# Attention with two exponential engines: loads by need, blank matmuls ahead of the scores, and longer VectorE chains from later jobs

## The chip, the cores and the metric

The kernel runs on one core of one Trainium2 chip. The metric is the device time of one execution in microseconds; lower is better. Before the change the median of 7 runs is 397.64 us (397.14 to 398.09).

## The reference

Grouped-query attention: 8 batches, 8 query heads, 2 key/value heads (each serves 4 query heads), 1024 positions, head size 64, float32 in and out.

```python
scores = scale * np.matmul(q_group, k_group.transpose(0, 1, 3, 2))
attn = np.exp(scores - np.max(scores, axis=-1, keepdims=True))
attn = attn / (np.sum(attn, axis=-1, keepdims=True) + 1e-08)
output[:, q_start:q_end, :, :] = np.matmul(attn, v_group)
```

The kernel leaves out the subtraction of the maximum (the scores are small) and the 1e-08.

## The kernel before, in words

**Jobs and cells.** A job is a batch, a head and a side: the even or the odd query rows of that head, 512 of them. There are 128 jobs, and each has 8 cells, one for each block of 128 keys: 1024 cells. A cell passes through a score matmul (128 keys by 512 queries, L351), an exponential, and four output matmuls (L414), which multiply the weights by V with a column of ones beside it, so that the sum of the weights comes out as a 65th column. When the eight cells of a job are done, `normalise` takes the reciprocal of that column (L427), multiplies (L429) and stores (L435, on SP's queue).

**Two ways to the exponential.** Cells of kind A go in pairs to ACT: one ACTIVATE over 128x1024 (L362). Cells of kind D go to DVE: L371 turns the score into the bits of a bfloat16 power of two, and when `GROUP` cells (four) have been gathered in one tile, a chain of four instructions over all of them mends the mantissa: an AND (L386), a line (L392), a product (L402) and an integer addition (L406). In PSUM, A has two slots of two banks, D two banks, and the outputs two banks; a bank is free again when its reader is done.

**The order.** `make_plan` plays the engines through with a table of costs and writes the order out: which score, exp, L371, chain step, output matmul and norm comes when. Each engine then runs its instructions strictly in that order, and waits by semaphores where data or a buffer isn't there. Cells are taken one after the other, the next one by whichever kind has a free bank first. Loads are put into the same list at due times before a head's first use (`first_use`).

**Loads.** `cast` (L248, POOL's queue) copies Q, K or V of a head from DRAM to a scratch in bfloat16, and is paced by a dependency on the latest score at that point of the list. `transpose` (L260, SP's queue) brings Q or K back transposed, in two pieces. `place_k` (L268, POOL's queue) copies the transposed K to the halves of `kset`; there K stands in one half of the partitions and zeros in the other, since `qT` holds the even rows in its lower and the odd rows in its upper half. There are two `kset`s, for even and odd batches; the zeros are set once, one set's by DVE (L236), the other's by POOL (L309). `place_v` (L282) is on SP's queue.

**The first head** (`first_loads`) takes a shorter way: K and Q come as float32 in one DMA each (L294), DVE casts K (L313, L314), ACT casts Q (L316), PE turns both (L321, L327), and DVE and ACT copy them from PSUM (L330 to L334).

Of the kernel before, what the change touches and what calls it, by code (L numbers as in the profile page):

```python
# [13 lines left out]

GROUP = 4


def make_plan(nj, nkc):
# [5 lines left out]

    QK, PV, EXP, P1, NORM = 0.214, 0.143, 0.925, 0.605, 0.57
    CHAIN = (0.73, 0.73, 1.26, 1.26)
    FROM_PE, FROM_ACT, FROM_DVE = 0.28, 0.18, 0.12
    LIVE_A, LIVE_D, PENDING, ONLY_A = 26, 6, 8, 14
    INF = 1e9
    n = nj * nkc  # L30
    ops = []
    pe = act = dve = 0.0
    a_free, bank, obank_free = [0.0, 0.0], [0.0, 0.0], [0.0, 0.0]
    nxt = 0
    open_jobs, next_job, rem, obank = [], 0, {}, {}
# [5 lines left out]
    a_id = d_id = -1  # L41

    def first_free(slots):
        return min(range(len(slots)), key=lambda s: slots[s])

    while normed < nj:
        best = None
        if nxt < n:
            ta = td = INF
            if open_a is not None:  # L50
                ta = max(pe, open_a["t"])
            elif live["A"] < LIVE_A:
                ta = max(pe, min(a_free))
            if pending < PENDING and nxt < n - ONLY_A and (cur or live["D"] < LIVE_D):
                td = max(pe, min(bank))
            t, to_d = (ta, 0) if ta <= td else (td, 1)
            if t < INF:
                best = min(best or (INF,), (t, 1 + to_d, "qk", to_d))
        for i, s in enumerate(open_jobs):
            for c in rem[s]:  # L60
                at = max(pe, ready.get(s * nkc + c, INF))
                if at < INF:
                    best = min(best or (INF,), (at, 3 + i, "pv", (s, c)))
        if len(open_jobs) < 2 and next_job < nj:
            at = max(pe, min(obank_free), min(ready.get(next_job * nkc + c, INF) for c in range(nkc)))
            if at < INF:
                best = min(best or (INF,), (at, 3 + len(open_jobs), "open", next_job))
        for q, p, kind in ((normq, 0, "norm"), (p1q, 1, "p1"), (chainq, 2, "chain")):
            if q:
                best = min(best or (INF,), (max(dve, q[0][0]), p, kind, 0))  # L70
        if cur and nxt >= n - ONLY_A and not p1q:
            best = min(best or (INF,), (dve, 9, "flush", 0))
        t, _, kind, arg = best
        if kind == "qk":
            cell = nxt
            nxt += 1
            pe = t + QK
            if not arg:
                if open_a is None:
# [8 lines left out]
                home[cell] = ("A", a_id)  # L88
                if len(o["cells"]) == 2 or nxt >= n:
                    act = max(act, pe + FROM_PE)  # L90
                    ops.append((act, "exp", a_id, tuple(o["cells"])))
                    act += EXP * len(o["cells"]) / 2
                    a_free[o["slot"]] = act + FROM_ACT
                    uses[("A", a_id)] = len(o["cells"])
                    for x in o["cells"]:
                        ready[x] = act + FROM_ACT
                    open_a = None
            else:
                k = first_free(bank)
                bank[k] = INF  # L100
# [44 lines left out]
        elif kind == "flush":  # L145
            chainq.append((dve, d_id, cur, 0))
            cur = []
        else:
            _, g, cells, step = chainq.pop(0)
            ops.append((t, "chain", g, len(cells), step))  # L150
            dve = t + CHAIN[step] * len(cells) / GROUP
            if step + 1 < len(CHAIN):
                chainq.insert(0, (dve, g, cells, step + 1))
            else:
                pending -= len(cells)
                uses[("D", g)] = len(cells)
                for x in cells:
                    ready[x] = dve + FROM_DVE
# [4 lines left out]
def kernel(  # L163
# [26 lines left out]
    E1 = D + 1  # L190
    PIECE = 256
    scale = 1.0 / math.sqrt(D)
    bits_scale = 128.0 * scale * math.log2(math.e)
# [13 lines left out]
    first_pool = ctx.enter_context(tc.tile_pool(name="firstp", bufs=1))  # L207
    qT_pool = ctx.enter_context(tc.tile_pool(name="qTpool", bufs=8))
    kT_pool = ctx.enter_context(tc.tile_pool(name="kTpool", bufs=4))
    pa_pool = ctx.enter_context(tc.tile_pool(name="papool", bufs=26))  # L210
    pd_pool = ctx.enter_context(tc.tile_pool(name="pdpool", bufs=6))
    tmp_pool = ctx.enter_context(tc.tile_pool(name="tmppool", bufs=2))
# [11 lines left out]
    apools, dbanks, obanks = psum_pools("aps", 2), psum_pools("dps", 2), psum_pools("ops", 2)  # L224

    ident = const_pool.tile([128, 128], BF16)
    make_identity(nc, ident)
    vsets, ksets = [], []
    for s in range(2):
# [4 lines left out]
        for side in range(2):  # L234
            if s == 0:
                nc.vector.memset(ks[(1 - side) * D : (2 - side) * D, :, side, :], 0.0)  # L236
        ksets.append(ks)
# [51 lines left out]
    def first_loads():  # L289

        staged = []
        for eng, src in ((nc.sync, k[0, 0]), (nc.scalar, q[0, 0])):
            f = first_pool.tile([128, NHC, 2, D], FP32, name=f"f{len(staged)}")
            eng.dma_start(  # L294
                out=f, in_=src.rearrange("(c p two) d -> p c two d", p=128, two=2)
            )
            staged.append(f)
        vf = first_pool.tile([128, NHC, 2, D], FP32, name="vf")
        nc.sync.dma_start(
            out=vf, in_=v[0, 0].rearrange("(c p two) d -> p c two d", p=128, two=2)  # L300
        )
        cast(("q", 0, 1), q[0, 1])
        for two in range(2):
# [3 lines left out]
            )  # L307
        for side in range(2):
            nc.gpsimd.memset(ksets[1][(1 - side) * D : (2 - side) * D, :, side, :], 0.0)  # L309
        fk, fq = staged  # L310

        hk = first_pool.tile([128, NHC, 3, D], BF16, name="hk")
        nc.vector.tensor_copy(out=hk[:, :, 0:2, :], in_=fk)  # L313
        nc.vector.tensor_copy(out=hk[:, :, 2, :], in_=fk[:, :, 0, :])  # L314
        hq = first_pool.tile([128, NHC, 2 * D], BF16, name="hq")
        nc.scalar.copy(out=hq, in_=fq.rearrange("p c two d -> p c (two d)"))  # L316
        tk = dbanks[0].tile([128, 2, HALF], BF16, name="dps0")
        tq = dbanks[1].tile([128, HALF], BF16, name="dps1")
        for w in range(2):
            for c in range(NHC):  # L320
                nc.tensor.transpose(  # L321
                    tk[:, w, c * 128 : (c + 1) * 128],
                    hk[:, c, w : w + 2, :].rearrange("p w d -> p (w d)"),
                    ident,
                )
        for c in range(NHC):
            nc.tensor.transpose(tq[:, c * 128 : (c + 1) * 128], hq[:, c, :], ident)  # L327
        qT[(0, 0)] = qT_pool.tile([128, HALF], BF16, name="qT")
        lo, hi = slice(0, D), slice(D, 2 * D)
        nc.vector.tensor_copy(out=ksets[0][lo, 0, 0, 0:HALF], in_=tk[lo, 0, :])  # L330
        nc.scalar.copy(out=qT[(0, 0)], in_=tq)
        nc.vector.tensor_copy(out=ksets[0][lo, 0, 0, HALF:S], in_=tk[lo, 1, :])
        nc.vector.tensor_copy(out=ksets[0][hi, 0, 1, 0:HALF], in_=tk[hi, 1, :])
        nc.vector.tensor_copy(out=ksets[0][hi, 0, 1, HALF:S], in_=tk[hi, 0, :])  # L334

# [113 lines left out]
    for op in plan:  # L449
        if op[1] == "qk":  # L450
            first_use.setdefault(op[2] // NKC, op[0])
        at(op[0], run[op[1]], *op[2:])
    for b in range(B):
        for h in range(H):
            if b == 0 and h == 0:
                continue
            th = first_use[(b * H + h) * 2]
            if (b, h) != (0, 1):
                at(th - 28.0, cast, ("q", b, h), q[b, h])
            for n in range(HALF // PIECE):  # L460
                at(th - 17.0 + n, transpose_q, b, h, n)
            if h % HPG == 0:
                g = h // HPG
                at(th - 38.0, cast, ("k", b, g), k[b, g])
                at(th - 33.0, cast, ("v", b, g), v[b, g])
                for n in range(HALF // PIECE):
                    at(th - 27.0 + n, transpose_k, b, g, n)
                for side in range(2):
                    for parity in range(2):
                        at(th - 20.0, place_k, b, g, side, parity)  # L470
                at(th - 15.0, place_v, b, g)
    with tc.manual_schedule():
# [33 lines left out]
```

The softmax here doesn't subtract the row's maximum and nothing guards it: scores larger than these inputs give would overflow.

## Time and profile before

| | us |
|---|---|
| median of 7 runs | 397.64 |
| the profiled execution | 397.68 |
| its span, first to last instruction | 395.9 |
| ACT busy | 381.5 |
| DVE busy | 376.0 |
| PE busy | 371.6 |
| POOL busy | 86.8 |
| first exp on ACT begins | 8.27 |
| last exp on ACT ends | 388.53 |

Busy times are sums over the profiled execution. A busy PE is not PE at its peak, since matmuls overlap and their ends are modelled. Lines of a timeline give the start, the time from the first instruction of the row to the end of its last, the engine, the line of the kernel, the operation, what it writes and reads, and how many instructions of the kind follow each other; in brackets is the idle time before the row and what ended it. Lines of a group give the busy time, the mean duration of one in ns, and the idle time before them. Lines of windows give the stretch and its length, then busy time and instructions of PE, PE's weight loads, DVE, ACT and POOL, then the granted clock of PE, the share of time that the DMA engines are busy, and GB/s.

### The profile page before, as it was taken

How to read it: one execution, taken by the hardware profiler on the slowest of the kernel's cores; microseconds unless marked ns; L12 is line 12 of the kernel's file. 1: busy time of each engine (PE TensorE's matmuls, PEld its weight loads, DVE VectorE, ACT ScalarE, POOL GpSimd, SP SyncE). 2: the span in 40 equal slices, each digit the busy share in tenths (PEclk: the TensorE clock that was granted, in tenths of full speed). 3: DMA queues.
4: the chain of work that ended last, by engine and by line, in shares of the span. 5: the costliest groups of instructions: out<-in, count | busy, mean ns of one | idle time of the engine just before them, and what ended most of it. 6: DMA issues, size and time to landing. Idle time of an engine off the chain costs nothing.

```text
span 395.9 us, 12772 instructions
## 1 busy us (share of the span) xinstructions
PE 371.6 (94%) x5132; PEld 232.9 (59%) x5132; DVE 376.0 (95%) x664; ACT 381.5 (96%) x415; POOL 86.8 (22%) x165
## 2 busy tenths in 40 slices
PE   4899999999999999999999999999999999999996
PEld 2455565565656656665656565565665666565655
DVE  4999999999999999999999999999999999999995
ACT  4999999999999999999999999999999999999992
POOL 5340403131041313113131040311213131120000
PEclk9999999999999999999999999999999999999999
DMA  4694967758586796857658576785965967564314
GB/s 106 106 141 89 164 112 140 133 102 135 100 133 124 119 150 113 134 96 137 117 106 137 104 150 119 128 128 98 160 107 112 156 127 118 108 126 97 68 28 94
DMA packets 134890, 46.72 MB, mean 118 GB/s; under 512 B 130848, under 2 KB 132384, under 8 KB 133344
## 3 DMA queue, kind: packets, MB, share of 16 engines
q1 hardware_dynamic: 129408, 29.52, 38.6%
q0 software_dynamic: 4896, 16.13, 27.0%
q8 instruction: 40, 0.66, 0.8%
q10 hardware_dynamic: 528, 0.26, 0.2%
q14 instruction: 18, 0.15, 0.1%
HBM read 27.13 MB, written 28.97 MB: 142 GB/s over the span
## 4 chain that ended last, share of the span: by engine, by line
ACT 71%; PE 9%; DVE 8%; issue 6%; DMA 4%; POOL 1%; SPq 1%
ACT pa L362 71%; PE aps L351 4%; PE ops L414 4%; DMA qT<-scr_q 2%; DVE y L402 2%; DVE pd L371 1%; DVE pd L406 1%; DVE ost L429 1%; DMA vf<-in_v_dram 1%; PE dps L351 1%; POOL kset L309 1%; DVE y L392 1%; DMA scr_q<-in_q_dram 1%; DVE z L386 1%; DVE rec L427 1%
## 5 line engine op out<-in xcount | busy, mean ns | idle before, releaser
L362 ACT ACTIVATE pa<-aps 128x1024 bf16<-128x1024 f32 x412 | 379.0, 1063 | 2.4 <-PE aps L351 1.6
L351 PE MATMUL aps<-qT,kset 128*128 128x512 bf16 x824 | 245.3, 379 | 14.0 <-ACT pa L362 11.9
L414 PEld LDWEIGHTS <-pa 128*128 128x128 bf16 x3296 | 134.6, 97 | 57.6 <-DVE ost L429 0.8
L414 PE MATMUL ops<-vset,pa 128*128 128x65 bf16 x3296 | 143.9, 193 | 0.0
L371 DVE TENSOR_SCALAR pd<-dps 128x512 uint16<-128x512 f32 x200 | 129.8, 682 | 2.3 <-PE dps L351 2.3
L351 PEld LDWEIGHTS <-kset 128*128 128x128 bf16 x1024 | 85.2, 97 | 66.4 <-issue 30.9
L248 POOL DMA_DIRECT2D scr_q<-in_q_dram x63 | 34.7, 550 | 174.8 <-PE aps L351 153.3
L351 PE MATMUL dps<-qT,kset 128*128 128x512 bf16 x200 | 64.5, 380 | 0.1
L406 DVE TENSOR_TENSOR pd<-pd,y 128x2048 uint16<-128x2048 uint16 x50 | 61.2, 1225 | 1.7
L402 DVE TENSOR_TENSOR y<-z,y 128x2048 f16<-128x2048 uint16 x50 | 61.2, 1225 | 1.7
L429 DVE TENSOR_TENSOR ost<-ops,rec 128x256 f32<-128x256 f32 x128 | 54.3, 425 | 4.4
L414 PEld LDWEIGHTS <-pd 128*128 128x128 bf16 x800 | 38.5, 97 | 30.0 <-DVE pd L406 8.1
L268 POOL DMA_DIRECT2D kset<-kT x60 | 31.9, 540 | 73.7 <-DMA kT<-scr_k 70.8
L414 PE MATMUL ops<-vset,pd 128*128 128x65 bf16 x800 | 45.3, 194 | 1.4 <-DVE pd L406 0.3
L392 DVE TENSOR_SCALAR y<-z 128x2048 f16<-128x2048 uint16 x50 | 34.3, 687 | 0.6
L386 DVE TENSOR_SCALAR z<-pd 128x2048 uint16<-128x2048 uint16 x50 | 34.3, 685 | 0.0
L427 DVE RECIPROCAL rec<-ops 128x4 f32<-128x4 f32 x128 | 22.5, 176 | 2.5 <-PE ops L414 1.9
L248 POOL DMA_DIRECT2D scr_k<-in_k_dram x15 | 8.1, 541 | 6.6 <-PE aps L351 5.7
L248 POOL DMA_DIRECT2D scr_v<-in_v_dram x15 | 7.5, 503 | 8.1 <-PE aps L351 7.0
L321 PE MATMUL dps<-ident,hk 128*128 128x128 bf16 x8 | 1.0, 308 | 5.1 <-DVE hk L313 5.1
L321 PEld LDWEIGHTS <-hk 128*128 128x128 bf16 x8 | 0.8, 138 | 5.1 <-DVE hk L313 5.1
L309 POOL MEMSET kset<- 64x2048 bf16 x2 | 3.6, 1798 | 0.1
(20 smaller groups left out, 9.7 us busy)
## 6 DMA issues: line engine op xcount, KB each, us to landing
out_dram<-ost SPq DMA_DIRECT2D x128, 128.0 KB, 3.1
scr_q<-in_q_dram POOLq DMA_DIRECT2D x63, 128.0 KB, 3.3
kset<-kT POOLq DMA_DIRECT2D x60, 64.0 KB, 2.7
qT<-scr_q SPq DMA_TRANSPOSE x126, 3.7
scr_k<-in_k_dram POOLq DMA_DIRECT2D x15, 128.0 KB, 4.2
scr_v<-in_v_dram POOLq DMA_DIRECT2D x15, 128.0 KB, 4.0
vset<-scr_v SPq DMA_DIRECT2D x30, 64.0 KB, 4.1
kT<-scr_k SPq DMA_TRANSPOSE x30, 3.2
```

The costliest lines, as they stand in the source:

```text
L248: dma = nc.gpsimd.dma_start(out=scr.rearrange("(p f) -> p f", f=1024), in_=src.rearrange("(p s) d -> p (s d)", s=1024 // D),)
L268: nc.gpsimd.dma_start(out=ksets[b % 2][side * D : (side + 1) * D, g, side, parity * HALF : (parity + 1) * HALF], in_=kT[(b, g)][parity * D ...
L351: last_score[0] = nc.tensor.matmul(dst, lhsT=ksets[b % 2][:, h // HPG, side, c * 128 : (c + 1) * 128], rhs=qT[(b, h)], start=True, stop=Tr ...
L362: nc.scalar.activation(out=pt[:, 0:m], in_=psum.pop(("A", n))[:, 0:m], func=AF.Exp, scale=scale)
L371: nc.vector.tensor_scalar(out=groups[g][:, slot], in0=psum.pop(cell), scalar1=bits_scale, scalar2=bits_bias, op0=ALU.mult, op1=ALU.add,)
L386: nc.vector.tensor_scalar(out=z, in0=pd, scalar1=0x7F, scalar2=None, op0=ALU.bitwise_and)
L392: nc.vector.tensor_scalar(out=y, in0=temps[g][0], scalar1=CURVE_A / 128.0, scalar2=CURVE_B, op0=ALU.mult, op1=ALU.add,)
L402: nc.vector.tensor_tensor(out=y, in0=z, in1=y, op=ALU.mult)
L406: nc.vector.tensor_tensor(out=pd, in0=pd, in1=y, op=ALU.add)
L414: nc.tensor.matmul(ops_of[s][:, qs, :], lhsT=p_of[cell][:, qs * 128 : (qs + 1) * 128], rhs=vsets[b % 2][:, h // HPG, c, :], start=opens an ...
L427: nc.vector.reciprocal(out=rec, in_=o[:, :, D])
L429: nc.vector.tensor_tensor(out=ost, in0=o[:, :, 0:D], in1=rec.unsqueeze(2).to_broadcast([128, NQS, D]), op=ALU.mult,)
```

## The change

- `GROUP` is 8: the four chain steps run over 4096 elements for each partition. There are 5 such tiles for 6 of the smaller ones, and 28 `pa` tiles for 26.
- The planner has new costs (a fixed part and a part for each cell). A cells are taken in the order of jobs; D cells are taken from jobs up to `LEAD` = 6 further on (fewer at the start), at most two of a job. A scores get precedence by 0.08 us in its clock. It counts on the loads of a head from a given time on.
- The first K and Q come in two DMAs each, and are cast, turned and copied by halves. 26 matmuls of a blank tile go ahead of the first transposes on PE, and two more between the halves. The third part of K's cast and the four transposes that need it come after the first copies to `kset`, still ahead of the first score.
- All four memsets of zeros are on DVE, at the start; POOL has none. The cast of the third head's Q goes out after the blank matmuls, paced by them.
- Loads have due times that are closer at the start and farther later, and the casts are sorted by them.

The order of the built kernel: 411 exps for 412, 202 cells on DVE for 200 (25 chains of eight cells and one of two, for 50 of four), 5160 matmuls for 5132.

```diff
-GROUP = 4
+GROUP = 8
...
-    QK, PV, EXP, P1, NORM = 0.214, 0.143, 0.925, 0.605, 0.57
-    CHAIN = (0.73, 0.73, 1.26, 1.26)
-    FROM_PE, FROM_ACT, FROM_DVE = 0.28, 0.18, 0.12
-    LIVE_A, LIVE_D, PENDING, ONLY_A = 26, 6, 8, 14
+    QK, PV, P1, NORM = 0.216, 0.1225, 0.603, 0.555
+    EXP, AND, LINE, PRODUCT = (0.065, 0.4265), (0.20, 0.133), (0.20, 0.133), (0.16, 0.27)
+    CHAIN = (AND, LINE, PRODUCT, PRODUCT)
+    FROM_PE, FROM_ACT, FROM_DVE, FROM_POOL = 0.26, 0.17, 0.10, 0.15
+    LIVE_A, LIVE_D, PENDING, PER_JOB, LEAD, RAMP, AHEAD, FIRST_PV = 28, 5, 16, 2, 6, 3, 0.08, 2.0
...
+        while job_a < nj and not todo[job_a]:
+            job_a += 1
+        lead = min(LEAD, job_a // RAMP)
+        job_d = max(job_d, job_a + lead)
+        while job_d < nj and (
+            taken[job_d] >= PER_JOB or not todo[job_d]
+        ):
+            job_d += 1
...
+                best = min(best or (INF,), (t - AHEAD, 1, "qk", 0, t))
+        if job_d < nj and job_d <= job_a + lead + 1 and pending < PENDING:
+            if cur or live["D"] < LIVE_D:
+                t = max(pe, min(bank), loaded(job_d))
...
+    blank = const_pool.tile([128, 128], BF16)
+    nc.vector.memset(blank, 0.0)
...
         for side in range(2):
-            if s == 0:
-                nc.vector.memset(ks[(1 - side) * D : (2 - side) * D, :, side, :], 0.0)
+            nc.vector.memset(ks[(1 - side) * D : (2 - side) * D, :, side, :], 0.0)
...
-        for side in range(2):
-            nc.gpsimd.memset(ksets[1][(1 - side) * D : (2 - side) * D, :, side, :], 0.0)
...
+        for eng, f, src in ((nc.sync, fk, k[0, 0]), (nc.scalar, fq, q[0, 0])):
+            for half in halves:
+                eng.dma_start(
+                    out=f[:, half], in_=src.rearrange(rows, p=128, two=2)[:, half]
+                )
...
+        last_score[0] = keep_warm(WARM)
+        for n, half in enumerate(halves):
+            nc.vector.tensor_copy(out=hk[:, half, 0:2, :], in_=fk[:, half])
+            nc.scalar.copy(
+                out=hq[:, half], in_=fq[:, half].rearrange("p c two d -> p c (two d)")
+            )
+            turn_k(0, half)
+            for c in range(NHC)[half]:
+                nc.tensor.transpose(tq[:, c * 128 : (c + 1) * 128], hq[:, c, :], ident)
+            if n == 0:
+                keep_warm(2)
+                cast(("q", 0, 2), q[0, 2])
+        for half in halves:
+            cols = slice(half.start * 128, half.stop * 128)
+            nc.scalar.copy(out=qT[(0, 0)][:, cols], in_=tq[:, cols])
+            put_k(0, 0, half)
+        nc.vector.tensor_copy(out=hk[:, :, 2, :], in_=fk[:, :, 0, :])
+        turn_k(1, slice(0, NHC))
+        put_k(0, 1, slice(0, NHC))
+        put_k(1, 0, slice(0, NHC))
+        put_k(1, 1, slice(0, NHC))
...
-                at(th - 28.0, cast, ("q", b, h), q[b, h])
+            spare = min(1.0, max(0.0, th - 10.0) / 50.0)
+                casts.append((th - 12.0 - 14.0 * spare, ("q", b, h), q[b, h]))
...
+    casts.sort(key=lambda e: e[0])
```

## The prediction

> **What bounds the kernel now.** I read the shares and the windows first, then the groups, then the timeline at both ends, where the windows show the slack.
>
> ```profile
> PE 371.6 (94%) x5132; PEld 232.9 (59%) x5132; DVE 376.0 (95%) x664; ACT 381.5 (96%) x415; POOL 86.8 (22%) x165
> ```
>
> ```profile
> 0.00:10.00 10.00, 4.24 (x20) 2.35 (x21) 4.42 (x9) 4.21 (x5) 5.55 (x13) 1.00 0.40 105
> ...
> 100.00:200.00 100.00, 96.74 (x1344) 61.05 (x1343) 97.46 (x172) 99.77 (x110) 22.26 (x41) 1.00 0.70 120
> ...
> 380.00:396.00 16.00, 11.07 (x225) 8.10 (x221) 11.09 (x22) 8.54 (x10) 0.00 (x0) 0.97 0.34 71
> ```
>
> The columns are PE, PEld, DVE, ACT, POOL. Three engines look full on average, but in the middle only ACT leaves nothing (99.77 of 100 us); DVE and PE wait for it. ACT is idle only at the ends. The groups give the prices:
>
> ```profile
> L362 ACT ACTIVATE pa<-aps 128x1024 bf16<-128x1024 f32 x412 | 379.0, 1063 | 2.4 <-PE aps L351 1.6
> ...
> L371 DVE TENSOR_SCALAR pd<-dps 128x512 uint16<-128x512 f32 x200 | 129.8, 682 | 2.3 <-PE dps L351 2.3
> ...
> L406 DVE TENSOR_TENSOR pd<-pd,y 128x2048 uint16<-128x2048 uint16 x50 | 61.2, 1225 | 1.7
> ```
>
> The exps start "8.3 to 387.4" by the view of their line: 379.1 us for 411 steps, 0.922 us each. So the span is a sum of three: 8.3 to the first exp, 379.1 from first to last exp start, 8.5 behind (395.9 - 387.4). The ends, in the timeline:
>
> ```profile
> 1.02 0.91 DVE L236 MEMSET kset<- 64x1024 uint32 x1 [1.02 <-PEq L490]
> ...
> 2.19 0.91 DVE L236 MEMSET kset<- 64x1024 uint32 x1 [0.25 <-issue]
> 4.60 0.43 DVE L313 CAST hk<-f 128x512 bf16<-128x512 f32 x1 [1.51 <-DMA f<-in_k_dram]
> ...
> 7.22 1.86 PE L351 MATMUL aps<-qT,kset 128*128 128x512 bf16 x4 [0.67 <-ACT qT L331]
> ...
> 8.27 2.96 ACT L362 ACTIVATE pa<-aps 128x1024 bf16<-128x1024 f32 x3 [1.10 <-PE aps L351]
> ...
> 386.75 0.60 PE L351 MATMUL aps<-qT,kset 128*128 128x512 bf16 x2
> ...
> 389.50 2.63 PE L414 MATMUL ops<-vset,pa 128*128 128x65 bf16 x80
> ...
> 392.38 0.42 DVE L429 TENSOR_TENSOR ost<-ops,rec 128x256 f32<-128x256 f32 x1
> ```
>
> K lands at 4.6, scores begin at 7.22 about 0.43 apart, and the last exp is followed by 4 us of output matmuls and norms, then a store (3.1 to land).
>
> **What the Trainium skill says.** "ScalarE: Activation LUTs", What ACT_TABLE_LOAD costs: one element per cycle, 186 ns + 0.833 ns per element, back-to-back overlap about 93. For 1024 that is 1039 alone and 946 in a row; the trace has 1063 and 922. Close: the pace is ACT's own, and no schedule shortens it. "VectorE: DVE Perf Modes", Side-by-side: where the cycles go for N=2048 bf16: 693 ns in the four-fold mode, 1224 in the two-fold, some 150 cycles of each being fixed. The trace agrees (685 and 687; 1225). "TensorE: Matmul & The Clock Gate", Part 1: The HAM clock gate (the "warmup" mystery): PE starts at half clock and is let up after about 3.4 us of work, 427 against 216 ns for 512 columns. The trace agrees: 0.43 apart at the start, later two in 0.59. "VectorE: DVE Perf Modes", Two Vector instructions with no wait between them: one whose output starts in another quadrant than the last waits for it to finish. The two memsets write different halves, and 0.26 us lie between them (1.93 to 2.19).
>
> **The change, part by part.**
>
> *Work on ACT.* The built order has 411 exps for 412 (822 cells, 202 on DVE): -0.9 us on the path. Nothing else shortens the middle.
>
> *Chains of eight.* Four steps of a four-cell chain cost 0.685+0.687+1.225+1.225 = 3.82, times 50 = 191.1. With the fixed 150 cycles paid once, 4096 elements cost 0.685+2048/3840 = 1.22 and 1.225+2048/1920 = 2.29 (estimates on the page's modes): 7.02 a chain, times 25 = 175.5, and one chain of two cells 2.2. DVE saves 13.4 and pays 1.4 for two more L371. It is worth nothing on the path: ACT hides it. What it costs is granularity: a product holds DVE 2.29, not 1.22, and norms (which free the two output banks) and L371 (which frees the two D banks) queue behind; PE, in order, may then stand before a D score or an output matmul with the next A score behind it. The A slots leave little: the last score pair ended at 387.35 and its exp began at 387.4. Bounds: -0.5 (the planner's costs now match the trace: L371 pitch 0.60, norm 0.55, so PE stands less) to +3; I take +0.4.
>
> *Start.* Four memsets now stand on DVE ahead of the first cast, with a blank of about 0.1. At the pitch seen (1.17) they end at 1.0+0.4+4x0.91+3x0.26 = 5.8; packed, 4.9. So K, though its first half lands before 4.6, is cast from about 5.9: halves of 0.29 (L314's 128x256), started 0.2 apart, done at 6.4. PE turns the second half until 6.75; DVE copies two halves (0.2 apart) and casts the third part, done at 7.45; PE then turns four more, which stand ahead of the first score, and scores from 7.7. Two warm scores end at 8.3: first exp 8.4. Cold would be 9.1, packed memsets 7.4. ACT's own way (Q by 5, a cast, two copies of half size) ends at about 7.2 and is hidden under DVE's. So the halves and the warm PE are spent on the memsets: +0.1, bounds -0.9 to +0.8.
>
> *Loads in order of need.* POOL loses 3.65 of memsets at 6.66 to 10.3, and head 2's cast goes out at about 4.2, not 10.27. The exps before 20 us lost about 0.5 (0.15 at 11.39, 0.39 at 19.33 for qT): -0.5. New risk: head 3's transposes now share SP's queue with K's at 1.2 to 1.6 us an issue and 3.7 to land; cast at about 8.5 they land near 18.5, when PE reaches that head's D score. Bounds 0 to +1.5, inside E below. Later the DMAs are the same in number and go out earlier or on due times; SP's stores and POOL's casts wait behind the same kinds of work, with buffers of 10 us: nothing.
>
> *The end.* After the last score pair, before had 144 output matmuls with norms between them; the changed order has 64. Eighty took 2.63, 0.033 each, so 2.1, then 0.1 and a norm of 0.63, then 3.1 to land: 5.9 after the last exp's start, for 8.5. -2.6 (bounds -3.0 and -1.8).
>
> Sum: 8.4 + (379.1-0.9-0.5+0.4 = 378.1) + 5.9 = 392.4 for 395.9. The profiled execution took 397.68 with 1.78 around its span, and the median is 397.64, so no shift: 392.4+1.8 = **394.2**.
>
> **Rivals.**
> - C, slower: the long products starve ACT. For: slack of about 0.1 us before each exp, two banks of each kind. Against: with four-cell chains of 1.22 PE never waited for DVE's D banks. Price: if each of the 50 steps of 2.29 passes on 0.2 us, +10: about 404. It decides from 3.5/50 = 0.07 us each. Chance 0.10.
> - D, DVE is the real bound: then its 12 us come out: 384. For: 95% busy. Against: ACT full in every middle window and as many exps as before. Chance 0.04.
> - E, the start eats it: PE cold (+0.7), loads late by 1.5 and twice more on later heads: 397.5. For: DVE's queue. Chance 0.12.
> - B, packed memsets and a clean run: 392.6. Chance 0.10.
> - A, the sum: 0.64.
>
> **How the numbers follow.** A measurement can tell 0.2% (0.8 us) from none: 396.8 and below is faster. A, B, D and a part of E give 0.82; C and a little of E 0.10 slower; 0.08 the same. The range goes from B with a better end, 391.8, to E's middle, 397.2.
>
> **What would show it.** First exp at 8.4 with DVE's casts after 5.5; 411 exps still at 0.917 to 0.922; 128x4096 rows at about 1.22 and 2.29; DVE busy about 365; under 6 us after the last exp's start. I am wrong if ACT shows idle behind PE aps in the middle by more than 2 us, if PE dps waits for DVE add up, or if the first exp comes before 7.3 or after 9.2.

## The result, and the profile after

| | before | after |
|---|---|---|
| median | 397.62 us (30 runs, 396.94 to 398.18) | 403.13 us (12 runs, 399.04 to 404.58) |
| the profiled execution | 397.68 | 402.26 |
| its span | 395.9 | 400.2 |
| first exp begins | 8.27 | 9.11 |
| from the first exp's start to the last's | 379.2 | 385.6 |
| from the last exp's start to the end | 8.5 | 5.5 |

The change made the kernel 1.2% slower: the ratio is 1.0123, 95% interval [1.0104, 1.0142]. The forecast was 394.2, at most 397.2. The end came out as expected; the time is lost in the middle, although there is one exp less. First the shares, then the windows (columns as before):

```profile
PE 369.6 (92%) x5160; PEld 232.8 (58%) x5160; DVE 368.8 (92%) x575; ACT 381.2 (95%) x416; POOL 91.0 (23%) x163
```

```profile
0.00:10.00 10.00, 6.59 (x45) 4.77 (x46) 5.97 (x13) 3.63 (x6) 3.35 (x13) 1.00 0.51 123
20.00:40.00 20.00, 14.86 (x174) 8.29 (x172) 16.34 (x22) 17.24 (x20) 8.89 (x17) 1.00 0.69 120
40.00:60.00 20.00, 17.44 (x217) 10.12 (x216) 17.72 (x28) 18.19 (x21) 5.21 (x11) 1.00 0.70 125
60.00:100.00 40.00, 35.61 (x506) 22.20 (x503) 35.90 (x56) 37.04 (x42) 8.04 (x13) 1.00 0.72 121
100.00:200.00 100.00, 97.18 (x1408) 62.21 (x1407) 96.88 (x151) 100.00 (x110) 24.69 (x42) 1.00 0.75 124
```

From 100 us on ACT is full, as before. Between 20 and 100 us it is 72.5 of 80. DVE is no busier there either (70.0), so it isn't DVE that holds ACT up. The timeline of ACT's exps shows the holes; the number in brackets is the idle time ahead of a row:

```profile
9.11 1.94 ACT L419 ACTIVATE pa<-aps 128x1024 bf16<-128x1024 f32 x2 [1.38 <-PE aps L408]
11.67 10.45 ACT L419 ACTIVATE pa<-aps 128x1024 bf16<-128x1024 f32 x11 [0.62 <-PE aps L408]
24.88 20.27 ACT L419 ACTIVATE pa<-aps 128x1024 bf16<-128x1024 f32 x22 [2.76 <-PE aps L408]
45.52 3.77 ACT L419 ACTIVATE pa<-aps 128x1024 bf16<-128x1024 f32 x4 [0.37 <-PE aps L408]
50.73 11.14 ACT L419 ACTIVATE pa<-aps 128x1024 bf16<-128x1024 f32 x12 [1.44 <-PE aps L408]
62.13 2.85 ACT L419 ACTIVATE pa<-aps 128x1024 bf16<-128x1024 f32 x3 [0.27 <-PE aps L408]
66.08 27.71 ACT L419 ACTIVATE pa<-aps 128x1024 bf16<-128x1024 f32 x30 [1.09 <-PE aps L408]
95.39 300.40 ACT L419 ACTIVATE pa<-aps 128x1024 bf16<-128x1024 f32 x327 [1.60 <-PE aps L408]
```

Six holes from 24.88 to 95.39 sum to 2.76 + 0.37 + 1.44 + 0.27 + 1.09 + 1.60 = 7.5 us; then 327 exps without one. ACT names only its neighbour, an A score of PE. What PE itself waited for stands in the view of the waits (us in total, times, longest):

```profile
PE aps L408 <- ACT pa L419: 14.0, 43, 0.7
...
PE dps L408 <- DMA qT<-scr_q: 8.2, 6, 3.1
...
PEld L408 <- DMA qT<-scr_q: 3.2, 3, 1.2
```

PE stood for 8.2 us ahead of D scores (`dps`) whose Q hadn't arrived. PE runs in a fixed order, so the A score behind such a D score is late, and ACT with it. A transpose itself lands no later after its issue than before (3.6 us in the median in both kernels); it is issued too late. The first hole in the timeline, with the rows between them left out:

```profile
11.93 0.49 POOL L279 DMA_DIRECT2D scr_q<-in_q_dram  x1 [2.50 <-PE aps L408]
...
17.62 1.70 SPq L291 DMA_TRANSPOSE kT<-scr_k  x1
...
19.37 1.85 SPq L291 DMA_TRANSPOSE qT<-scr_q  x1
...
24.04 0.38 PE L408 MATMUL dps<-qT,kset 128*128 128x512 bf16 x1 [3.10 <-DMA qT<-scr_q]
...
24.88 1.02 ACT L419 ACTIVATE pa<-aps 128x1024 bf16<-128x1024 f32 x1 [2.76 <-PE aps L408]
```

The third head's cast leaves POOL at 11.93. Its second transpose is issued by SP at 19.37, behind one of K. PE has waited since 20.9 and goes on at 24.04; the exp follows at 24.88.

The cause lies in two parts of the diff together. D cells are taken up to three heads (six jobs) ahead of the A cells, so the first use of a head moves forward: in the planner's order from 47.2 to 35.7 for head 8, from 70.9 to 52.3 for head 12. And the loads are due closer to the first use: at the start a cast 12 us ahead of it for 28, a transpose 7 for 17, growing to nearly the old values only at 60 us (`spare`). In the trace the second transposes, which end a head's load, came hardly earlier than before:

| head (us) | before: cast issued, second transpose's issue ends | after | old due times (experiment below) |
|---|---|---|---|
| 3 | 11.3, 22.2 | 11.9, 21.2 | 7.6, 17.3 |
| 8 | 27.7, 46.2 | 30.5, 46.8 | 21.0, 36.5 |
| 12 | 50.9, 66.6 | 42.6, 66.4 | 34.1, 55.3 |

So the use moved and the load didn't, or by far less. My theory: the time is lost to Q's loads (L), and within that to due times that are too short for this order (D). Rivals: the lookahead itself, which grows faster than SP can transpose whatever the due times (S); the spacing between casts; and, for the start, the memsets (M), which leave PE cold.

### The profile page after: what moved, and what is told of

Its sections match the earlier page's. It is cut to its first block, busy times and chain, and to the rows that moved or that the text cites. A ratio compares the mean times of both kernels' runs of the same rounds, so it can differ in the third digit from the quotient of the medians.

```text
span 400.2 us, 12716 instructions
## 1 busy us (share of the span) xinstructions
PE 369.6 (92%) x5160; PEld 232.8 (58%) x5160; DVE 368.8 (92%) x575; ACT 381.2 (95%) x416; POOL 91.0 (23%) x163
## 4 chain that ended last, share of the span: by engine, by line
ACT 70%; PE 13%; DMA 7%; issue 6%; DVE 3%; SPq 1%; ACTq 0%
ACT pa L419 70%; PE aps L408 7%; DMA qT<-scr_q 6%; PE ops L471 3%; PE dps L408 2%; SPq L291 1%; DVE kset L267 1%; DMA scr_q<-in_q_dram 1%; DVE pd L428 1%; DVE pd L463 1%; DMA out_dram<-ost 0%; PE dps L352 0%; DVE ost L486 0%; DVE kset L361 0%; SPq L492 0%
## 5 line engine op out<-in xcount | busy, mean ns | idle before, releaser
L471 PE MATMUL ops<-vset,pa 128*128 128x65 bf16 x3288 | 148.8, 194 | 0.0
L408 PE MATMUL dps<-qT,kset 128*128 128x512 bf16 x202 | 71.2, 382 | 8.5 <-DMA qT<-scr_q 8.2
L463 DVE TENSOR_TENSOR pd<-pd,y 128x4096 uint16<-128x4096 uint16 (+1 forms) x26 | 57.8, 2224 | 0.3
L459 DVE TENSOR_TENSOR y<-z,y 128x4096 f16<-128x4096 uint16 (+1 forms) x26 | 57.7, 2221 | 0.1
L299 POOL DMA_DIRECT2D kset<-kT x60 | 36.9, 624 | 54.0 <-DMA kT<-scr_k 43.6
L471 PE MATMUL ops<-vset,pd 128*128 128x65 bf16 x808 | 41.3, 193 | 0.0
L484 DVE RECIPROCAL rec<-ops 128x4 f32<-128x4 f32 x128 | 22.7, 178 | 12.7 <-PE ops L471 11.4
L449 DVE TENSOR_SCALAR y<-z 128x4096 f16<-128x4096 uint16 (+1 forms) x26 | 31.1, 1195 | 0.0
L443 DVE TENSOR_SCALAR z<-pd 128x4096 uint16<-128x4096 uint16 (+1 forms) x26 | 30.9, 1187 | 0.0
L267 DVE MEMSET kset<- 64x1024 uint32 x4 | 3.6, 912 | 1.0 <-issue 1.0
L339 PE MATMUL ops<-blank 128*128 128x128 bf16 x28 | 3.4, 313 | 1.0 <-DVE blank L257 1.0
```

Source lines behind the costliest of these rows:

```text
L299: nc.gpsimd.dma_start(out=ksets[b % 2][side * D : (side + 1) * D, g, side, parity * HALF : (parity + 1) * HALF], in_=kT[(b, g)][parity * D ...
L408: last_score[0] = nc.tensor.matmul(dst, lhsT=ksets[b % 2][:, h // HPG, side, c * 128 : (c + 1) * 128], rhs=qT[(b, h)], start=True, stop=Tr ...
L443: nc.vector.tensor_scalar(out=z, in0=pd, scalar1=0x7F, scalar2=None, op0=ALU.bitwise_and)
L449: nc.vector.tensor_scalar(out=y, in0=temps[g][0], scalar1=CURVE_A / 128.0, scalar2=CURVE_B, op0=ALU.mult, op1=ALU.add,)
L459: nc.vector.tensor_tensor(out=y, in0=z, in1=y, op=ALU.mult)
L463: nc.vector.tensor_tensor(out=pd, in0=pd, in1=y, op=ALU.add)
```

## The experiments

Each ratio is to the kernel before, with its 95% interval.

**No Q loads.** Q isn't loaded after the first head; every score reads that head's `qT`.

```diff
-            rhs=qT[(b, h)],
+            rhs=qT[(0, 0)],
...
-                casts.append((th - 12.0 - 14.0 * spare, ("q", b, h), q[b, h]))
-            for n in range(HALF // PIECE):
-                at(th - 7.0 - 10.0 * spare + n, transpose_q, b, h, n)
+                pass
```

> This kernel leaves out the loads of Q behind the first head (63 casts, 126 transposes): every score takes the first head's qT. The order of PE, ACT and DVE is that of the changed kernel. Theory L (PE stands before D scores of later heads whose Q has not landed): the idle of ACT between 20 and 95 us, some 9 us, goes, and the time is about 393 to 394. Rival P (the long products of DVE, or the planned order itself, starve ACT): the idle stays, time 400 or more.

Measured: 393.99 (393.74 to 394.27), ratio to before 0.9913 [0.9898, 0.9927]. ACT's last row of exps:

```profile
11.68 375.84 ACT L417 ACTIVATE pa<-aps 128x1024 bf16<-128x1024 f32 x409 [0.62 <-PE aps L406]
```

409 exps in a row. All of the loss, 9.1 us in the medians (403.13 to 393.99), goes with the loads of Q; chains of eight and the new order cost ACT nothing by themselves.

**Slower lookahead.** The lead grows by one job every 8 jobs, for every 3.

```diff
-    LIVE_A, LIVE_D, PENDING, PER_JOB, LEAD, RAMP, AHEAD, FIRST_PV = 28, 5, 16, 2, 6, 3, 0.08, 2.0
+    LIVE_A, LIVE_D, PENDING, PER_JOB, LEAD, RAMP, AHEAD, FIRST_PV = 28, 5, 16, 2, 6, 8, 0.08, 2.0
```

> The one number RAMP is 8 for 3, so that D cells run ahead by a job more after every 8 jobs, not after every 3; exps (411) and chains stay as many. Theory S (the load path of SP's queue already runs at the pace of consumption, so each head of lookahead has to be gained, and the steep lookahead asks for more than it can give): the stalls before 95 us shrink from 9.5 to under 3, time about 396. Rival D (the due times, which are counted from the first use, are simply too short at the start): first uses move and due times with them, so most of the stalls stay, time 400 or more.

Measured: 400.38, 401.12 and 402.69, ratio 1.0099 [1.0071, 1.0126]. This is what D expected (400 or more) and not what S did (about 396): a slower growth removes hardly any time. The one execution that was profiled took 409.02, far above these three, so where the holes lie isn't read from it.

**Old due times.** The changed kernel, its start and its order, with the due times of before: Q 28 us ahead (transposes 17), K 38, V 33, without sorting and spacing.

```diff
-                casts.append((th - 12.0 - 14.0 * spare, ("q", b, h), q[b, h]))
+                at(th - 28.0, cast, ("q", b, h), q[b, h])
...
-                at(th - 7.0 - 10.0 * spare + n, transpose_q, b, h, n)
+                at(th - 17.0 + n, transpose_q, b, h, n)
```

> The plan and the start of the changed kernel with the due times of the kernel before (cast 28, transposes 17 ahead of first use, K 38 and 27). Rival D: the Q of the lookahead heads comes earlier, stalls shrink to under 3, time about 395. Theory S: SP's queue is full in either case, only the order on it changes, and the stalls stay within 3 us of 9.5: time 399 to 405.

Measured: 394.7 (393.9 to 395.01), ratio 0.9927 [0.9912, 0.9942]. ACT:

```profile
8.89 1.94 ACT L419 ACTIVATE pa<-aps 128x1024 bf16<-128x1024 f32 x2 [1.67 <-PE aps L408]
11.21 2.85 ACT L419 ACTIVATE pa<-aps 128x1024 bf16<-128x1024 f32 x3 [0.39 <-PE aps L408]
14.44 372.89 ACT L419 ACTIVATE pa<-aps 128x1024 bf16<-128x1024 f32 x406 [0.37 <-PE aps L408]
```

No hole after 14.44, and PE's wait for Q at D scores falls from 8.2 us to this:

```profile
PE dps L408 <- DMA qT<-scr_q: 0.3, 1, 0.3
```

D holds; S falls in the form that I gave it, since the same lookahead runs without a stall when the loads start earlier. SP issued 28 transposes in the first 50 us, against 21 in the changed kernel and 21 in before: 13 against 10 up to 25 us, and 15 against 11 behind that.

**Casts unspaced.** Is it the spacing of the casts rather than the short leads?

```diff
-    CAST_GAP = 3.0
+    CAST_GAP = 0.0
...
-        soonest = t + 2.0
+        soonest = t
```

> The changed kernel with only the spacing of the casts taken out (CAST_GAP 0, no two microseconds between two casts); the short due times at the start stay. If the spacing is what makes the first heads late (the third head's cast waits until 11.9 with it), the stalls go and the time is about 395, as with the old due times. If the short leads are (transposes 7 ahead of use in place of 17), the stalls stay near 9 us: 401 to 404. In between: both.

Measured: 402.88, ratio 1.0122 [1.0068, 1.0176]. Behind 20 us there are holes of 7.4 us, for 7.5. The spacing made the hole at 24.88: the third head's cast now goes out at 9.45, and ACT runs on to 42.3. But the later heads lose what is gained, 4.6 us at one place (65.07). So the short leads lose as much time without the spacing.

**Memsets later.** For the start: the second `kset`'s zeros are set by DVE in four pieces from 20 us on, and 34 blank matmuls fill PE until K is there.

```diff
-            nc.vector.memset(ks[(1 - side) * D : (2 - side) * D, :, side, :], 0.0)
+            if s == 0:
+                nc.vector.memset(ks[(1 - side) * D : (2 - side) * D, :, side, :], 0.0)
...
+    for n in range(4):
+        at(20.0 + 2.0 * n, blank_k, n // 2, n % 2)
...
-    WARM = 26
+    WARM = 34
```

> Only the start: the second kset's zeros are set in four pieces on DVE from about 20 us on and not ahead of the first cast, and 34 blank matmuls stand for 26, so that PE has no gap before the first transposes. Theory M (the memsets hold the first cast of K until 5.5, and the gap of PE from 3.95 to 5.81 keeps it cold): casts begin by 4.5, the first exp at about 7.3 with warm scores, 1.8 us earlier than in the changed kernel. Rival: PE stays cold whatever is put ahead, first exp at about 8. The whole time falls by less than 1.8 if the loads set the pace behind it, since then the stalls grow by what the start gains.

Measured: 400.54 (398.62 to 403.56), ratio 1.0093 [1.0067, 1.012]. The start of the changed kernel, then of this one:

```profile
0.99 2.96 PE L339 MATMUL ops<-blank 128*128 128x128 bf16 x26 [0.99 <-DVE blank L257]
...
4.69 0.91 DVE L267 MEMSET kset<- 64x1024 uint32 x1 [0.25 <-issue]
...
5.53 0.42 DVE L368 CAST hk<-fk 128x256 bf16<-128x256 f32 x2
...
5.81 0.39 PE L352 MATMUL dps<-ident,hk 128*128 128x128 bf16 x2 [1.86 <-DVE hk L368]
...
8.02 1.91 PE L408 MATMUL aps<-qT,kset 128*128 128x512 bf16 x4
```

```profile
3.62 0.29 DVE L369 CAST hk<-fk 128x256 bf16<-128x256 f32 x1 [0.34 <-DMA fk<-in_k_dram]
...
6.66 1.03 PE L409 MATMUL aps<-qT,kset 128*128 128x512 bf16 x3
...
7.29 1.02 ACT L420 ACTIVATE pa<-aps 128x1024 bf16<-128x1024 f32 x1 [0.74 <-PE aps L409]
```

In the changed kernel the cast waits for the fourth memset, PE idles 1.86 us after its blank matmuls, and four scores take 1.91 (0.43 apart: cold). Here the first cast is at 3.62, scores follow each other in 0.22 (7.09 and 7.31; of the four in the row the trace has three), and the first exp begins at 7.29 for 9.11. M is right on the start, 1.8 us. But 7.3 us of holes stay behind the first exp (8.2 in the changed kernel): the start isn't what was lost.

**Half as many transposes.** The short due times stay; each head's Q, and each K, is transposed by one DMA instead of two.

```diff
-    PIECE = 256
+    PIECE = 512
```

> The changed kernel with PIECE 512 for 256: one DMA transpose per head in place of two of half the size, so SP issues 78 for 156; due times and order as in the changed kernel. If SP's time per issue (1.5 us a transpose, 22 to 24 of 25 us in use) is what keeps a late load late, SP has 4 us of 25 or more to spare and the stalls fall from 9.5 to under 4: time under 398. If the transposes take their time by bytes, or the short leads alone are the cause, the time stays at 400 to 404.

Measured: 394.0 (393.62 to 394.95), ratio 0.9897 [0.9876, 0.9918]. ACT:

```profile
9.11 377.46 ACT L419 ACTIVATE pa<-aps 128x1024 bf16<-128x1024 f32 x411 [1.37 <-PE aps L408]
```

All 411 exps in one row, with nothing changed in the due times. (The hole at 11.67 is gone for another reason: with the same start, the last cold score began at 8.44 in this execution and at 11.43 in the changed kernel's.) SP's row says why the later ones are. The view of the transposes' line gives the shortest, median and longest issue in ns, in before, in the changed kernel and in this one:

```profile
L260 SPq DMA_TRANSPOSE qT<-scr_q x126: 1103/1237/3575, 6.3 to 366.4; - x126
```

```profile
L291 SPq DMA_TRANSPOSE qT<-scr_q x126: 1103/1236/3552, 5.4 to 362.3; - x126
```

```profile
L291 SPq DMA_TRANSPOSE qT<-scr_q x63: 1122/1491/3567, 5.5 to 347.5; - x63
```

A transpose of twice the size holds SP a fifth longer, so a head costs SP 1.5 us for 2.5. Landing takes 4.0 for 3.7. Head 8 shows what stood in the way. In the changed kernel its cast had landed at 33.8, but its two transposes went out 9 and 12 us later; here the cast landed at 30.9 and the one transpose went out at 32.68. The two of the changed kernel, then the one of this run:

```profile
42.84 1.36 SPq L291 DMA_TRANSPOSE qT<-scr_q  x1
...
45.66 1.18 SPq L291 DMA_TRANSPOSE qT<-scr_q  x1
```

```profile
32.68 1.76 SPq L291 DMA_TRANSPOSE qT<-scr_q  x1
```

Sums of SP's DMA instructions by the stretch in which they start, with whatever they wait inside, in us:

| stretch | before | after | old due times | half as many | stores off SP |
|---|---|---|---|---|---|
| 0 to 25 | 14.9 | 18.0 | 20.1 | 13.1 | 17.7 |
| 25 to 50 | 22.9 | 23.9 | 24.0 | 20.8 | 25.0 |
| 50 to 75 | 23.0 | 22.2 | 22.0 | 14.1 | 22.5 |
| 75 to 100 | 24.7 | 22.7 | 23.4 | 17.0 | 16.8 |

From 25 us on SP's queue was already occupied nearly all the time before the change, which nothing on the page's shares tells, since issues aren't counted as busy there. Occupied isn't the same as at a fixed limit. At the shortest issue seen of each kind, the 22 instructions of before between 25 and 50 us would take 16.5 us (an estimate: 11 transposes of 1.1, 8 stores of 0.37, 3 loads of V of 0.46), and with the old due times SP issued 15 transposes in that stretch where the changed kernel issued 11. What makes single issues longer, up to 3.6 us, isn't shown. What the runs show is that the lead is there when the loads are placed earlier on the queue (old due times), or when the queue has less to issue (this run).

**Stores off SP.** The other way to relieve it: the outputs are stored from POOL's queue.

```diff
-        nc.sync.dma_start(
+        nc.gpsimd.dma_start(
             out=out[b, h].rearrange("(s p two) d -> two p s d", p=128, two=2)[side],
```

> The changed kernel with the stores issued on POOL's queue and not on SP's, which takes some 0.6 us a store, about a fifth, off SP. If a full SP queue keeps late loads late, the stalls fall by half or more, time under 399. If not, 400 to 404; POOL's casts now wait behind stores, which could add to it.

Measured: 398.35 (395.75 to 400.27), ratio 0.9998 [0.9981, 1.0014]: half of the loss. In the profiled execution (400.12) it takes 381.8 us from the first exp to the last, for 385.6, and the end is longer, 7.2 for 5.5.

```profile
25.35 1.02 ACT L419 ACTIVATE pa<-aps 128x1024 bf16<-128x1024 f32 x1 [3.00 <-PE aps L408]
...
28.76 363.26 ACT L419 ACTIVATE pa<-aps 128x1024 bf16<-128x1024 f32 x395 [0.18 <-PE aps L408]
```

The hole near 25 us stays, since no store has been issued by then; from 28.76 on there is none. A store waits on SP for DVE, with the transposes behind it: the one issued at 44.29 in the changed kernel held SP for 1.32 us, 0.53 in the median. This is what the Trainium skill says in "DMA: Bandwidth & Descriptors", Anatomy of one DMA — SWDGE (gpsimd) path: any semaphore wait happens on the sequencer that issues the DMA, before it is sent. The trace agrees, for DMAs from SP. Between 25 and 100 us, where the holes are, such waits of stores on DVE sum to 5.2 us; the rest of what SP is spared there is the issue of 19 stores.

**The new start alone.** The kernel before with the whole `first_loads` of the changed one (halves, blank matmuls, memsets on DVE, the third head's cast early), and with its own planner, chains of four and due times.

```diff
+    blank = const_pool.tile([128, 128], BF16)
+    nc.vector.memset(blank, 0.0)
...
-            if s == 0:
-                nc.vector.memset(ks[(1 - side) * D : (2 - side) * D, :, side, :], 0.0)
+            nc.vector.memset(ks[(1 - side) * D : (2 - side) * D, :, side, :], 0.0)
...
-        for side in range(2):
-            nc.gpsimd.memset(ksets[1][(1 - side) * D : (2 - side) * D, :, side, :], 0.0)
...
+        last_score[0] = keep_warm(WARM)
...
+                cast(("q", 0, 2), q[0, 2])
```

> The kernel before with the new first loads, the blank matmuls and all memsets on DVE; the old planner, chains of four, old due times. By the changed kernel's trace the first exp comes at 8.9 to 9.1 for 8.27 and the next two are late by another 0.5 to 0.9; against that the loads of the third head come 6 us earlier, which saves up to 0.5. Expected 0.5 to 1.5 slower than before: 398.1 to 399.1. Rival (the warm PE and halves gain as meant): 396.5 or less.

Measured: 396.62 (396.13 to 397.33), ratio 0.9971 [0.9959, 0.9983]. This missed: I expected slower. The first exp is 0.9 us later (9.16), as in the changed kernel, but from first to last exp it takes 377.9 for 379.2, with 410 exps in a row from 11.72. Part of that is the hole of 0.39 at 19.33 in before, which the early cast removes. Another part are six exps in before, 64 exps apart, each about 0.25 late though a slot was free; they don't occur here. Their cause isn't settled.

**Chains of four.** With the old due times: are the chains of eight needed?

```diff
-GROUP = 8
+GROUP = 4
...
-    LIVE_A, LIVE_D, PENDING, PER_JOB, LEAD, RAMP, AHEAD, FIRST_PV = 28, 5, 16, 2, 6, 3, 0.08, 2.0
+    LIVE_A, LIVE_D, PENDING, PER_JOB, LEAD, RAMP, AHEAD, FIRST_PV = 28, 10, 16, 2, 6, 3, 0.08, 2.0
...
-    pd_pool = ctx.enter_context(tc.tile_pool(name="pdpool", bufs=5))
+    pd_pool = ctx.enter_context(tc.tile_pool(name="pdpool", bufs=10))
```

> The old due times with chains of four (GROUP 4, ten pd tiles); lookahead, start and costs of the changed kernel. The planner then gives DVE 196 cells and ACT 414 exps for 411. Theory N (the length of a chain is worth nothing but what it does to the number of exps): three exps more at 0.92, time 394.7+2.8 = 397.5. Theory G (long products starve ACT, so short ones free it): less than 396. Theory V (DVE is the bound): DVE has some 12 us more of work, time 401 or more.

Measured: 398.98 (397.94 to 403.43), ratio 1.004 [1.0019, 1.0061]: 4.3 above the same kernel with chains of eight, nearest to N but 1.5 over it. In its profiled execution the exps (414 for 411) explain 2.3 us from first to last, the later first exp 0.2, and the end 1.9 (7.4 for 5.5): after the last scores PE waits for DVE's chain:

```profile
391.48 0.67 PE L471 MATMUL ops<-vset,pd 128*128 128x65 bf16 x16 [1.19 <-DVE pd L463]
```

So chains of eight gain some 4 us here, by their fewer exps and by the end.

**Two edits together.** Old due times and later memsets, as above, then the same with the planner told to count on each head's loads 2 us later (`FIRST_LOAD`).

```diff
-    FIRST_LOAD, EACH_LOAD = 3.5, 4.0
+    FIRST_LOAD, EACH_LOAD = 5.5, 4.0
```

> The old due times and the later memsets with 34 blank matmuls together. With the loads early the gain of the start is no longer given back: first exp at about 7.3 for 8.9, no more than 1 us of stalls behind it, time about 393.0 (394.7 less 1.6). If the earlier start only meets later loads, 394.5 or more.

> The old due times and the later memsets, with FIRST_LOAD 5.5 for 3.5: the planner takes the loads to come 2 us later, which is what the earlier start took from them. It then has 412 exps. If the older start's loads were just in time and the earlier first exp (7.3 for 8.9) overran them, the stalls go and the time is 393.5 to 394.5; if the earlier memsets or the 34 blank matmuls hurt in another way, it stays at 396 to 398.

Measured: 397.12 (395.19 to 399.86), ratio 0.9984 [0.9967, 1.0001], and 396.29 (394.61 to 396.74), ratio 0.9943 [0.9922, 0.9963]. Both missed. The first exp came at 7.53 in the first, 1.4 us before that of the old due times alone, yet the holes were back: 4.2 us behind the first exp, for 0.8. PE waits 2.7 for Q at D scores. Another 1.2 of the holes (at 33.73 and 40.27) isn't Q: there PE waits for DVE, soon after the late memsets on it. The gains don't add: a start that is earlier by 1.4 us asks for the next heads' Q earlier by as much, and these loads don't come earlier. Counting on them later takes back a part: PE's waits for Q fall to 0.3 in the profiled execution, which was the fastest of its six (394.61).

**All three.** Old due times and later memsets with 34 blank matmuls, as above, and whole transposes.

```diff
-    PIECE = 256
-    WARM = 26
+    PIECE = 512
+    WARM = 34
```

> The old due times, the memsets later with 34 blank matmuls, and whole transposes. If SP's issues are what took the start's gain back with the old due times and later memsets (397.1 for 394.7), SP has room now: first exp at 7.1 to 7.5, no stall over 1 us behind it, time 392.0 to 393.0. If the first heads' loads are late by their latency and not by SP's issues, stalls of 1 to 3 us stay before 45 us: 394 to 396.

Measured: 393.65 (393.19 to 394.91), ratio 0.9909 [0.9892, 0.9926], between my two forecasts. With the transposes halved, the early start (first exp at 7.09) keeps: PE waits for no Q. ACT:

```profile
7.09 2.92 ACT L420 ACTIVATE pa<-aps 128x1024 bf16<-128x1024 f32 x3 [0.68 <-PE dps L353]
...
38.43 348.13 ACT L420 ACTIVATE pa<-aps 128x1024 bf16<-128x1024 f32 x379 [0.77 <-PE aps L409]
```

The hole at 38.43 follows a wait of PE for DVE's D bank (1.05 us, at 37.53), soon after the four late memsets on DVE (26.6 to 34.7). It beats both kernels; against whole transposes alone (394.0) it is no gain that these runs can tell.

## Why the prediction was wrong, step by step

- *Loads in order of need*: this step failed. It said "Later the DMAs are the same in number and go out earlier or on due times; SP's stores and POOL's casts wait behind the same kinds of work, with buffers of 10 us: nothing", and for head 3 "Bounds 0 to +1.5, inside E". Measured: where -0.5 stood, and nothing for later heads, Q that came too late cost holes of 7.5 us in the profiled execution, 9.1 in the medians (changed kernel against no Q loads). I compared the loads with their own due times, and not with the new first uses, and I left out SP's queue, which was occupied nearly all the time in the trace of before. "Buffers of 10 us" counted tiles for Q, where the turn on SP was what came late. For head 3 the cast was put at about 8.5; it went out at 11.93, with the spacing (9.45 without), and its Q landed at 23.9 and not near 18.5.
- *Rival E* named the place, late loads and a cold PE, but priced it at 397.5. Its +0.7 for a cold PE came. Its term "twice more on later heads" was the right kind; six holes came, the first of them 2.76 where I had bounded it by 1.5.
- *Start*: 8.4, measured 9.11. The memsets ended at 5.60 (5.8 predicted), halves and casts went as described, but PE was cold: the scores began at 8.02 for 7.7, and were 0.43 apart (the "Cold would be 9.1" of the text). The Trainium skill, "TensorE: Matmul & The Clock Gate", What's actually happening, asks for about 3.4 us of sustained work. The blank matmuls ran 2.96 us and were followed by 1.86 us of idling, and the trace agrees that this was too little. With 34 and no such gap the scores were warm. Which of the two did it, the length or the gap, no run here separates.
- *Work on ACT*: right. 411 exps, 0.917 apart.
- *Chains of eight*: right. 128x4096 took 1218, 1226, 2282 and 2286 ns (1.22 and 2.29 predicted), DVE is busy for 368.8 (about 365), and rival C fell:

```profile
PE dps L408 <- DVE pd L428: 0.2, 1, 0.2
```

  One wait of 0.2 us for DVE's D banks in the whole kernel; +0.4 for granularity isn't seen.
- *The end*: right. 5.5 us behind the last exp's start (5.9 predicted, 8.5 before). PE's last A scores, and the first 32 of the 64 output matmuls behind them, which end at 396.6:

```profile
394.03 0.59 PE L408 MATMUL aps<-qT,kset 128*128 128x512 bf16 x2
...
394.46 1.15 PE L471 MATMUL ops<-vset,pa 128*128 128x65 bf16 x32
...
396.85 0.42 DVE L486 TENSOR_TENSOR ost<-ops,rec 128x256 f32<-128x256 f32 x1
```

- *The sum*: start +0.7, first to last exp 385.6 for 378.1 (+7.5), end -0.4, around the span +0.3 (2.1 for 1.8) is +8.1, and 394.2 + 8.1 = 402.3, the profiled execution. With the loads relieved (half as many transposes) the sum stands: 394.0.
- My sign that I'd be wrong, ACT idle behind PE by over 2 us in the middle, is what came. The runs also scatter more (5.5 us from lowest to highest, 1.2 before). That fits DMA landing times on the path, but no run shows it by itself.

## What to carry to other kernels

When work is reordered so that data are used earlier, put the new first use of each tile beside the time at which its load lands in the trace, and look at the issuing queue as at an engine: SP had no busy share on the page, and was occupied nearly all the time. Each of three things gave a lead here: loads placed earlier on the queue, fewer and larger DMAs, and, in part, stores with waits taken off it. Remedies at the start and in the loads don't add up while one queue bounds both.

## What the runs showed of the hardware that wasn't expected

- A DMA transpose of Q with 512 rows held SP for 1491 ns in the median, one with 256 rows 1236; the shortest of each were 1122 and 1103. Halving their number gained 9.1 us in the medians.
- 2.96 us of matmuls on zeros and then 1.86 us of idling left PE cold: the next scores were 0.43 apart. How long differs with the same start: the last score that took over 0.6 us, for 0.38, began at 11.4 or 11.5 in five traces, at 9.7 with chains of four and at 8.4 with whole transposes. 3.81 us without such a gap had it warm (0.22 apart) at some time between 5.2 and 7.1 in four traces.
- Two memsets on DVE that write different halves of the partitions are 0.25 us apart, three times of three, as the prediction took it from one such pair. No run has two on the same half to compare.
